# Two transformer blocks on one core: both tiles' x transposed unscaled, x^T of the first stage loaded as a second layout

## The chip, the cores and the metric

One core of one Trainium2 chip runs the whole program in one launch. The metric is the device time in microseconds, the median of three runs. The engines are named as in the profile: PE (TensorE) multiplies, PEld is its weight load, DVE (VectorE) and ACT (ScalarE) do elementwise work, POOL (GpSimd) a few small operations, and SP (SyncE) issues all DMAs, in order, on one queue.

## The reference

The input x has 256 tokens of width 1024, float32. It goes through two layers of a hybrid block and then two layers of a second block. Every sublayer has the same frame: a root mean square norm with a gain, one or more projections, some work of its own, an output projection, another norm with a gain, and the residual sum.

```python
def rms_norm(x, gain):
    xf = x.astype(jnp.float32)
    y = xf * lax.rsqrt(jnp.mean(xf * xf, axis=-1, keepdims=True) + EPS)
    return (y * gain.astype(jnp.float32)).astype(x.dtype)

def hybrid_layer(...):                      # two of these
    h = rms_norm(x, attn_pre_gain)
    u = h @ w_in                            # 4120 columns: q, k, v of two attentions, gates
    ...                                     # rope, sliding window attention with sinks, sparse attention
    mixed = sigmoid(g_a) * (o_a @ w_branch_a) + sigmoid(g_b) * (o_b @ w_branch_b)
    x = x + rms_norm(mixed @ w_out, attn_post_gain)
    h = rms_norm(x, ffn_pre_gain)
    x = x + rms_norm(conv_ffn(h, ...), ffn_post_gain)   # up 5632, causal conv of 3, gelu(a) * v, down
    return x

def second_block(...):                      # two layers of this
    f = _swiglu(_rmsnorm(x, g[0]), ...);  x = x + 0.5 * _rmsnorm(f, g[1])
    m = _mixer(_rmsnorm(x, g[2]), ...);   x = x + _rmsnorm(m, g[3])     # attention, short conv, pooling
    f = _swiglu(_rmsnorm(x, g[4]), ...);  x = x + 0.5 * _rmsnorm(f, g[5])
```

## The kernel before

The 256 tokens are two tiles of 128, called t = 0 and t = 1. There are ten stages: attention and FFN of layer 0 and 1, and then FFN, mixer, FFN of each layer of the second block. Both tiles go through all stages, the first a few weight units ahead of the second, so that the first tile's work of a stage fills PE while the second tile ends the stage before.

A product in float32 accuracy is made of three products of a fast format: each operand is split in a high part (a rounding copy on ACT) and a low part (the difference on DVE), and high x high, high x low and low x high are summed (`mm3`, lines 736 to 740). Weights come in units of 128 x 1024 float32 (512 KB): a DMA into one of three `raw` buffers, then `wh` on ACT and `wl` on DVE, into one of nine pairs (`loader`, `unit`).

A stage needs x^T, the model dimension on the partitions, as eight blocks `kt` of 128. `proj` uses x^T as the stationary operand and 512 weight columns as the moving one: eight blocks of three products for each tile. `proj_c` makes **joint products**: the weights stay, and both tiles' x^T, 256 columns, high and low side by side in the tile `xj`, move past them (lines 1508 and 1509). Since the norm's factor 1/rms belongs to a token, a product of `proj` can take it later, when its result leaves the accumulator (ACT's `scale`); a joint product has both tokens' tiles in its columns and needs x^T with 1/rms in it.

In the eight stages with joint products (`whole`: both FFNs and the mixer) the two tiles are made ready in two ways. Of the first tile x is transposed as it is as soon as it is written (`x_t`, line 787 does the transposing), goes into `xt[0]` as high and low, and feeds `proj`; beside that 1/rms is transposed to a row (line 857), and `times_row` makes x^T times 1/rms in `xj`. Of the second tile `x_normed` first makes 1/rms (two squares with sums on ACT, a power on POOL, line 776), multiplies x by it (line 513), and then transposes that straight into `xj`, from which both kinds of products read. In the attention stages both tiles are transposed as they are.

The program starts with loads of x in halves of 256 KB, of `first` (identity for the transposes, rope frequencies, gains) and of the first weights; PE begins with the sixteen transposes of x.

No engine's order is written out by hand. While the program is built, a planner (`_Order`) runs the stages as generators with a clock of its own: every instruction has an engine, a cost in a formula and a rank, and of those that are ready an engine takes the one of lowest rank. Ranks of this change: the transposes of x 1 to 1.3, 1/rms 1.5, `times_row` 3.2, a weight unit 4.5 or 7 by how soon it is needed, joint products 6. What comes out is fixed: on the chip each engine runs its list in order and waits for semaphores.

## Time and profile before

| | |
|---|---|
| median of 3 runs | 1708.73 us (1706.84 to 1711.24) |
| the profiled execution | 1708.78 us |
| its span, first to last instruction | 1706.8 us |
| instructions of PE, DVE, ACT, POOL | 8920, 2966, 2436, 56 |
| loaded | 302.26 MB, mean 177 GB/s |

A busy share is time in which an engine's rows cover the span. PE's rows overlap, since a product starts before the one in front has ended; the distance from start to start is what one more product costs. A wait is listed with what ended it. An instruction's idle time is what its engine stood still in front of it, so where PE waits the idle time and the distance of the two starts say nearly the same.

### The profile page before, as it was taken

How to read it: one execution, taken by the hardware profiler on the slowest of the kernel's cores; microseconds unless marked ns; L12 is line 12 of the kernel's file. 1: busy time of each engine (PE TensorE's matmuls, PEld its weight loads, DVE VectorE, ACT ScalarE, POOL GpSimd, SP SyncE). 2: the span in 40 equal slices, each digit the busy share in tenths (PEclk: the TensorE clock that was granted, in tenths of full speed). 3: DMA queues.
4: the chain of work that ended last, by engine and by line, in shares of the span. 5: the costliest groups of instructions: out<-in, count | busy, mean ns of one | idle time of the engine just before them, and what ended most of it. 6: DMA issues, size and time to landing. Idle time of an engine off the chain costs nothing.

```text
span 1706.8 us, 25832 instructions
## 1 busy us (share of the span) xinstructions
PE 1677.7 (98%) x8920; PEld 1391.8 (82%) x8920; DVE 1295.6 (76%) x2966; ACT 1078.6 (63%) x2436; POOL 40.5 (2%) x56
## 2 busy tenths in 40 slices
PE   8999999999999999999999999999999999999998
PEld 6778888888778888888888787888788887778887
DVE  7996898887977988896667878666776669776664
ACT  6665776677665866675556677555655556865553
POOL 0000000001000000000000000000000000000000
PEclk9999999999999999999999999999999999999999
DMA  7436555565246555556566545555665555446553
GB/s 242 156 103 219 177 182 184 187 202 180 94 147 192 173 185 189 191 180 203 165 195 198 173 148 174 176 183 191 201 186 163 192 189 178 154 160 193 178 185 111
DMA packets 85380, 302.26 MB, mean 177 GB/s; under 512 B 9984, under 2 KB 10240, under 8 KB 85248
## 3 DMA queue, kind: packets, MB, share of 16 engines
q1 hardware_dynamic: 85248, 300.60, 54.0%
q8 instruction: 70, 1.15, 0.3%
q14 instruction: 62, 0.51, 0.1%
HBM read 299.51 MB, written 1.05 MB: 176 GB/s over the span
## 4 chain that ended last, share of the span: by engine, by line
PE 77%; DVE 11%; DMA 5%; ACT 5%; issue 2%; POOL 0%; SPq 0%; DVEq 0%; POOLq 0%; ACTq 0%
PE bank L1508 24%; PE bank L1509 12%; PE bank L740 12%; PE bank L738 12%; PE bank L739 12%; DVE wl L502 4%; DMA raw<-in_w_dram 4%; DVE b L502 2%; PE bank L787 2%; ACT b L493 2%; ACT wh L493 2%; DVE x L506 1%; PE bank L1243 1%; ACT junk L493 1%; PE bank L1181 1%
## 5 line engine op out<-in xcount | busy, mean ns | idle before, releaser
L502 DVE TENSOR_TENSOR wl<-raw,wh 128x512 fp32r<-128x512 f32 x1096 | 721.6, 687 | 93.9 <-ACT wh L493 77.6
L493 ACT ACTIVATE wh<-raw 128x512 fp32r<-128x512 f32 x1096 | 641.9, 624 | 139.8 <-DMA raw<-in_w_dram 83.6
L1508 PE MATMUL bank<-xj,wh 128*128 128x512 f32 x1856 | 655.3, 397 | 2.1 <-ACT b L493 2.1
L1509 PE MATMUL bank<-xj,wl 128*128 128x256 f32 x1856 | 482.8, 281 | 0.0
L1508 PEld LDWEIGHTS bank<-xj,wh 128*128 128x128 f32 x1856 | 339.5, 188 | 69.3 <-ACT b L493 3.0
L1509 PEld LDWEIGHTS bank<-xj,wl 128*128 128x128 f32 x1856 | 350.1, 189 | 23.7
L493 ACT ACTIVATE b<-bank 128x256 f32<-128x256 f32 (+3 forms) x304 | 126.1, 418 | 302.6 <-PE bank L1508 278.7
L502 DVE TENSOR_TENSOR b<-b,bank 128x256 f32<-128x256 f32 x232 | 97.7, 421 | 207.5 <-ACT b L493 205.0
L738 PE MATMUL bank<-wh,r 128*128 128x512 f32 x528 | 208.7, 395 | 0.0
L740 PE MATMUL bank<-wh,r 128*128 128x512 f32 x528 | 206.3, 391 | 0.7 <-DVE r L502 0.6
L739 PE MATMUL bank<-wl,r 128*128 128x512 f32 x528 | 205.9, 390 | 0.0
L738 PE MATMUL bank<-wh,xj 128*128 128x512 f32 x400 | 165.9, 415 | 0.2
L740 PE MATMUL bank<-wh,xj 128*128 128x512 f32 x400 | 157.9, 395 | 1.8 <-DVE xj L506 1.8
L739 PE MATMUL bank<-wl,xj 128*128 128x512 f32 x400 | 156.8, 392 | 0.0
L738 PE MATMUL bank<-wh,xh 128*128 128x512 f32 x336 | 135.3, 403 | 0.0
L740 PE MATMUL bank<-wh,xl 128*128 128x512 f32 x336 | 131.8, 392 | 0.4 <-DVE xl L506 0.4
L739 PE MATMUL bank<-wl,xh 128*128 128x512 f32 x336 | 130.9, 390 | 0.0
L740 PEld LDWEIGHTS bank<-wh,r 128*128 128x128 f32 x528 | 99.1, 188 | 24.2 <-DVE r L502 2.7
L739 PEld LDWEIGHTS bank<-wl,r 128*128 128x128 f32 x528 | 99.3, 188 | 19.2
L738 PEld LDWEIGHTS bank<-wh,r 128*128 128x128 f32 x528 | 99.2, 188 | 18.3 <-ACT r L493 1.2
L740 PEld LDWEIGHTS bank<-wh,xj 128*128 128x128 f32 x400 | 75.4, 188 | 21.2 <-DVE xj L506 4.6
L493 ACT ACTIVATE r<-b 128x256 fp32r<-128x256 f32 (+1 forms) x128 | 55.6, 438 | 58.1 <-DVE b L502 40.5
(140 smaller groups left out, 1665.1 us busy)
## 6 DMA issues: line engine op xcount, KB each, us to landing
raw<-in_w_dram SPq DMA_DIRECT2D x547, 512.0 KB, 3.4
gp<-in_post_dram SPq DMA_DIRECT2D x10, 512.0 KB, 4.5
b<-in_w_dram SPq DMA_DIRECT2D x16, 256.0 KB, 5.5
x<-in_x_dram SPq DMA_DIRECT2D x4, 256.0 KB, 5.3
out_dram<-x SPq DMA_DIRECT2D x4, 256.0 KB, 2.0
small<-in_small_dram SPq DMA_DIRECT2D x1, 858.0 KB, 5.2
raw<-in_w_dram SPq DMA_DIRECT2D x2, 256.0 KB, 3.8
c<-in_const_dram SPq DMA_DIRECT2D x1, 292.0 KB, 4.2
```

Source lines behind the costliest of these rows:

```text
L493: return _Op("act", cost, lambda: self.nc.scalar.activation(out, in_, func, **kw), table or TABLE_OF.get(func))
L502: return _Op("dve", 0.069 + 0.00104 * _n(out), lambda: self.nc.vector.tensor_tensor(out, a, b, op=op))
L506: return _Op("dve", cost, lambda: self.nc.vector.scalar_tensor_tensor(out, in0=in0, scalar=scalar, in1=in1, op0=op0, op1=op1))
L738: mm(out, lhsT=ah, rhs=bh, start=start, stop=False)
L739: mm(out, lhsT=ah, rhs=bl, start=False, stop=False)
L740: mm(out, lhsT=al, rhs=bh, start=False, stop=stop)
L787: self.nc.tensor.transpose(ps[:, j * P:(j + 1) * P], s, self.ident)
L1181: nc.tensor.matmul(sb[i][:, 256 * k:256 * k + 256].rearrange("p (c k) -> p c k", c=2), lhsT=q[a][gs, j * P:(j + 1) * P], rhs=b[gs, br, slots],
L1243: nc.tensor.matmul(o[gs, oc:oc + 256], lhsT=vc, rhs=pT, start=n == 0 and c == 0, stop=br == 0 and n == chain[0] - 1 and c == 1)
L1508: both = lambda: nc.tensor.matmul(ps, lhsT=wh[:, c], rhs=self.xj2[:, kt], start=kt == 0, stop=kt == KT - 1)
L1509: low = lambda: nc.tensor.matmul(ps[:, 256:512], lhsT=wl[:, c], rhs=self.xj[0][:, kt], start=False, stop=False)
```

## The change

The second tile gets the first tile's way. `x_normed` and `scale` go; `x_t` transposes x as it is for both tiles into `xt[t]`; `proj` reads `xt[t]`; the evacuations of both tiles multiply by 1/rms and wait for it; the row of 1/rms and `times_row` are made for both tiles, of rank 2.8 now. The mixer's conv and pool parts, which write into `xt` later, wait for the input products of both tiles.

At the start x^T is a second input, laid out on the host as [128, 2048]. Four pieces of 256 KB are loaded and multiplied by the gain straight into `xj`, so that attention's first stage has no transposes of x; x itself is loaded behind them, for the norm and the residual. The gains come alone and first. PE gets eleven products on a zeroed tile, whose result nobody reads, in front of its first work. Three numbers of the planner are others: a DMA's landing 3.0 instead of 2.0, the power 0.95 instead of 0.6, and the loads of the post gains are put off by 40 or 20.

```diff
 def _layout(x):
+    a["xt"] = np.ascontiguousarray(a["x"].reshape(2, P, KT, P).transpose(3, 0, 2, 1).reshape(P, 2 * D))
...
-        self.row = self.sb([P, P], F32, "row")
+        self.row = self.sb([P, 2, P], F32, "row")
...
     def dma(self, out, in_, cost=0.1):
-        return _Op("dma", cost, lambda: self.nc.sync.dma_start(out=out, in_=in_), late=2.0)
+        return _Op("dma", cost, lambda: self.nc.sync.dma_start(out=out, in_=in_), late=3.0)
...
     def first_loads(self):
-        x(0, 0, 0)
-        order.go(load(self.first, self.d["first"], 0.45, "first"), 0.1)
-        x(0, 1, 0.3)
-        x(1, 0, 0.4)
-        x(1, 1, 0.6)
+        def x_t(t, h):
+            b = yield from self.one("b")
+            yield self.dma(b, self.d["xt"][:, D * t + 512 * h:D * t + 512 * h + 512], 0.73)
+            yield ("ev", "pre")
...
+                    yield self.cpa(self.xj[0][:, kt, s], src(kt), gain(kt))
...
+                    yield self.stt(self.xj[1][:, kt, s], src(kt), gain(kt), self.xj[0][:, kt, s].bitcast(F32),
+                                   ALU.mult, ALU.subtract)
...
+        def warm():
+            ps = yield from self.one("tr")
+            yield self.mset(self.junk, 0.0)
+            for _ in range(11):
+                yield self.pe(0.44, lambda: self.nc.tensor.matmul(ps, lhsT=self.junk[:, 0:P], rhs=self.junk,
+                                                                  start=True, stop=True))
+            self.free("tr", ps)
+        order.go(load(self.first[:, 0:10 * KT], self.d["first"][:, 0:10 * KT], 0.2, "pre"), 0)
+        order.go(x_t(0, 0), 0.2)
+        order.go(warm(), 0.1)
+        order.go(x_t(1, 0), 0.4)
+        order.go(x_t(0, 1), 0.55)
+        order.go(x_t(1, 1), 0.65)
+        order.go(load(self.first[:, 10 * KT:], self.d["first"][:, 10 * KT:], 0.3, "first"), 0.9)
+        x(0, 0.8)
+        x(1, 0.95)
...
     def norm_t(self, t, dst, gi, name, whole=False):
-        if whole and t:
-            self.order.go(self.x_normed(t, dst, gi, name), 1)
-            return
-        for q in range(4):
+        for q in range(4) if name != ("attn", 0) else ():
             self.order.go(self.x_t(t, q, dst, gi, name), 1 + 0.1 * q)
...
-                yield self.cp(self.row, ps[:, 0:P])
+                yield self.cp(self.row[:, t], ps[:, 0:P])
                 self.free("tr", ps)
                 for h in range(2):
-                    self.order.go(self.times_row(h, name), 3.2)
+                    self.order.go(self.times_row(t, h, name), 2.8)
...
-    def x_normed(self, t, dst, gi, name):
-        m = yield from self.one("m")
-        xn = yield self.get("b", 2)
...
-        yield from self.rstd(m)
-        for h in range(2):
-            yield self.ts(xn[h], half(h), m[:, 3:4])
-            self.order.set((name, "xn", t, h))
...
     def ffn_tile(self, l, i, t):
-        lhs = self.lhs_j(self.xj, t) if t else self.lhs_t(self.xt[0])
+        lhs = self.lhs_t(self.xt[t])
...
-            self.post_gain(n)
+            self.post_gain(n, 40.0)
...
     def glu_in(self, l, i, t, c, ps):
-        if t == 0:
-            yield ("ev", (name, "rs", t))
-        yield self.act(s[:, 0:256], ps[:, 0:256], AF.Silu, scale=self.scale(t))
-        yield self.stt(s[:, 256:512], ps[:, 256:512], self.scale(t), s[:, 0:256], ALU.mult, ALU.mult)
+        yield ("ev", (name, "rs", t))
+        yield self.act(s[:, 0:256], ps[:, 0:256], AF.Silu, scale=self.rs[t][:, 0:1])
+        yield self.stt(s[:, 256:512], ps[:, 256:512], self.rs[t][:, 0:1], s[:, 0:256], ALU.mult, ALU.mult)
...
     def mix_joint(self, l):
-            yield ("ev", (name, "in", 0, 2))
+            for t in range(2):
+                yield ("ev", (name, "in", t, 2))
...
-            self.order.go(self.loader(), lambda: (0.2, 0.5)[self.loaded] if self.loaded < 2 else 2)
+            self.order.go(self.loader(), lambda: (0.3, 0.5, 0.6, 0.7)[self.loaded] if self.loaded < 4 else 2)
```

What this does to the lists of the engines is shown at three places. The first is SP's list at the very start; x_122 and x_123 are the two tiles of x, raw_100 to raw_102 the weight buffers, and 128x512 of float32 are 256 KB. Before:

```order
1 L535 DMA x_122<-in_x_dram 128x512
2 L535 DMA first<-in_first_dram 128x272
3 L535 DMA raw_100<-in_w_dram 128x512 x2
4 L535 DMA x_122<-in_x_dram 128x512
5 L535 DMA x_123<-in_x_dram 128x512
6 L535 DMA raw_101<-in_w_dram 128x1024
7 L535 DMA x_123<-in_x_dram 128x512
8 L535 DMA pos<-in_positions_dram 128x1 x2
9 L535 DMA raw_102<-in_w_dram 128x1024
10 L535 DMA raw_100<-in_w_dram 128x1024
```

And now, with the pieces of x^T in the working buffers b_69 to b_72:

```order
1 L537 DMA first<-in_first_dram 128x80
2 L537 DMA b_69<-in_xt_dram 128x512
3 L537 DMA raw_100<-in_w_dram 128x512 x2
4 L537 DMA b_70<-in_xt_dram 128x512
5 L537 DMA raw_101<-in_w_dram 128x1024
6 L537 DMA b_71<-in_xt_dram 128x512
7 L537 DMA raw_102<-in_w_dram 128x1024
8 L537 DMA b_72<-in_xt_dram 128x512
9 L537 DMA x_122<-in_x_dram 128x1024
10 L537 DMA raw_100<-in_w_dram 128x1024
11 L537 DMA first<-in_first_dram 128x192
12 L537 DMA x_123<-in_x_dram 128x1024
```

The loads of x stand behind three weight units, and the fourth unit, the identity and the positions stand behind the first load of x.

The second place is PE's list where the second tile enters the mixer of the second block's first layer. r_88 feeds its last output product of the FFN in front, rs_129 and rs_130 are 1/rms of the two tiles, xh_125 and xl_126 the first tile's x^T, wh and wl weights, and b_79 and b_80 are the second tile's x times 1/rms. Before:

```order
4329 L740 MATMUL bank_62<-wh_119,r_88 128x512
4330 L857 MATMUL bank_66<-first,rs_129 128x128
...
4349 L787 MATMUL bank_65<-first,b_77 128x128 x4
...
4364 L740 MATMUL bank_63<-wh_109,xl_126 128x512
4365 L787 MATMUL bank_61<-first,b_79 128x128 x2
4366 L787 MATMUL bank_66<-first,b_79 128x128 x2
4367 L738 MATMUL bank_63<-wh_109,xh_125 128x512
...
4370 L787 MATMUL bank_67<-first,b_80 128x128 x2
4371 L738 MATMUL bank_64<-wh_111,xj 128x512
```

And now, where x_123 is the second tile's x, xh_127 its x^T, and line 1525 (1508 before) a joint product:

```order
4357 L785 MATMUL bank_64<-wh_103,r_88 128x512
...
4370 L832 MATMUL bank_63<-first,b_81 128x128 x4
...
4376 L785 MATMUL bank_66<-wh_117,xl_126 128x512
4377 L832 MATMUL bank_67<-first,x_123 128x128 x2
4378 L832 MATMUL bank_62<-first,x_123 128x128 x2
4379 L783 MATMUL bank_66<-wh_115,xh_125 128x512
...
4382 L832 MATMUL bank_61<-first,x_123 128x128 x2
...
4408 L832 MATMUL bank_63<-first,b_69 128x128 x4
4409 L890 MATMUL bank_67<-first,rs_130 128x128
...
4437 L785 MATMUL bank_62<-wh_117,xl_128 128x512
4438 L1525 MATMUL bank_66<-xj,wh_103 128x512
```

The second tile's transposes stand 18 products behind its last output product instead of 33; a second transpose of 1/rms is there, and 27 products later the first joint product.

The third place is DVE's list in the same stage change; m_98 and m_93 are the second tile's mean square before the power. Before:

```order
1722 L513 TENSOR_SCALAR m_98<-m_98 128x1
1723 L502 TENSOR_TENSOR xj<-b_76,xj 128x4x128
1724 L502 TENSOR_TENSOR b_75<-b_75,row 128x512
1725 L513 TENSOR_SCALAR b_79<-x_123,m_98 128x512
1726 L502 TENSOR_TENSOR wl_120<-raw_102,wh_119 128x512
1727 L513 TENSOR_SCALAR b_80<-x_123,m_98 128x512
1728 L502 TENSOR_TENSOR xj<-b_75,xj 128x4x128
1729 L502 TENSOR_TENSOR wl_120<-raw_102,wh_119 128x512
1730 L506 SCALAR_TENSOR_TENSOR xj<-bank_61,first,xj 128x128
```

And now, from the same point, with b_77 and b_80 the two halves of the second tile's x^T:

```order
1758 L515 TENSOR_SCALAR m_93<-m_93 128x1
...
1768 L519 COPY row<-bank_67 128x128
1769 L504 TENSOR_TENSOR wl_120<-raw_101,wh_119 128x512
1770 L504 TENSOR_TENSOR b_77<-xh_127,xl_128 128x512
1771 L504 TENSOR_TENSOR b_80<-xh_127,xl_128 128x512
1772 L504 TENSOR_TENSOR b_77<-b_77,row 128x512
1773 L504 TENSOR_TENSOR b_80<-b_80,row 128x512
1774 L504 TENSOR_TENSOR wl_120<-raw_101,wh_119 128x512
1775 L504 TENSOR_TENSOR wl_108<-raw_102,wh_107 128x512
1776 L519 COPY b_70<-bank_61 128x512
1777 L504 TENSOR_TENSOR xj<-b_77,xj 128x4x128
1778 L504 TENSOR_TENSOR xj<-b_80,xj 128x4x128
```

The two passes over x (b_79, b_80) are gone, and between the row and the second tile's xj stand two sums, two products and two differences, with weight passes among them.

## Rows read from the trace of the kernel before

**Rows 1.** The page, part 1: engine, busy us (share of the span), instructions
```profile
PE 1677.7 (98%) x8920; PEld 1391.8 (82%) x8920; DVE 1295.6 (76%) x2966; ACT 1078.6 (63%) x2436; POOL 40.5 (2%) x56
```

**Rows 2.** Waits of PE: engine, line, what ended them: us, times, longest
```profile
PE bank L787 <- DVE b L513: 5.6, 7, 1.4
PE bank L787 <- DMA first<-in_first_dram: 4.4, 1, 4.4
PE bank L787 <- DVE b L506: 4.0, 2, 2.2
PE bank L787 <- DMA x<-in_x_dram: 2.4, 1, 2.4
...
PE bank L740 <- DVE xj L506: 1.8, 5, 0.6
```

**Rows 3.** Timeline of the start: start, us, engine, line, tiles [idle before]
```profile
4.37 1.09 PE L787 MATMUL bank<-first,x 128*128 128x128 f32 x4 [4.37 <-DMA first<-in_first_dram]
...
5.07 1.31 ACT L493 ACTIVATE xj<-bank,first 128x128 fp32r<-128x128 f32 x4 [2.83 <-PE bank L787]
...
7.83 1.54 PE L787 MATMUL bank<-first,x 128*128 128x128 f32 x6 [2.38 <-DMA x<-in_x_dram]
...
9.03 0.78 PE L738 MATMUL bank<-wh,xj 128*128 128x512 f32 x1
...
9.60 0.63 PE L739 MATMUL bank<-wl,xj 128*128 128x512 f32 x1
...
12.87 0.74 PE L738 MATMUL bank<-wh,xj 128*128 128x512 f32 x1
...
13.44 0.40 PE L739 MATMUL bank<-wl,xj 128*128 128x512 f32 x1
```

**Rows 4.** Windows: length, PE, PEld, DVE, ACT, POOL busy, clock, DMA share
```profile
0.00:10.00 10.00, 3.26 (x12) 2.73 (x13) 2.31 (x7) 5.31 (x14) 0.20 (x4) 1.00 0.76 260
10.00:20.00 10.00, 10.00 (x41) 8.14 (x40) 9.71 (x35) 8.42 (x23) 1.10 (x2) 1.00 0.76 277
...
50.00:60.00 10.00, 9.09 (x71) 6.38 (x70) 8.49 (x31) 6.33 (x12) 0.00 (x0) 1.00 0.90 320
```

**Rows 5.** Chain of waits between 0 and 130 us: start us, us, what
```profile
44.68 5.42 DMA raw<-in_w_dram
...
53.84 5.49 DMA b<-in_w_dram
```

**Rows 6.** Timeline of a stage change of the second tile, 942 to 953 us
```profile
942.74 0.39 PE L740 MATMUL bank<-wh,r 128*128 128x512 f32 x1
...
946.88 0.75 DVE L506 SCALAR_TENSOR_TENSOR x<-b,m,x 128x512 f32<-128x512 f32 x1
...
948.14 0.74 DVE L506 SCALAR_TENSOR_TENSOR x<-b,m,x 128x512 f32<-128x512 f32 x1
...
950.36 1.46 POOL L776 TENSOR_TENSOR m<-m,half 128x1 f32<-128x1 f32 x1 [4.19 <-DVE m L513]
...
950.73 0.69 DVE L502 TENSOR_TENSOR b<-b,row 128x512 f32<-128x512 f32 x1
950.85 0.39 PE L740 MATMUL bank<-wh,xl 128*128 128x512 f32 x1
...
951.86 0.49 DVE L513 TENSOR_SCALAR b<-x,m 128x512 f32<-128x512 f32 x1 [0.44 <-POOL m L776]
...
952.40 0.66 PE L787 MATMUL bank<-first,b 128*128 128x128 f32 x4 [1.17 <-DVE b L513]
```

**Rows 7.** Instructions on the tile row: ns min/median/max, first and last start
```profile
L502 DVE TENSOR_TENSOR b<-b,row x16: 680/683/689, 198.5 to 1521.0; 128x512 f32<-128x512 f32 x16
L517 DVE COPY row<-bank x8: 279/282/286, 196.3 to 1516.4; 128x128 f32<-128x128 f32 x8
```

**Rows 8.** Line 857: the same columns
```profile
L857 PE MATMUL bank<-first,rs x8: 271/271/272, 195.6 to 1515.5; 128*128 128x128 f32 x8
```

**Rows 9.** Instructions on the tile x: the same columns
```profile
L513 DVE TENSOR_SCALAR b<-x,m x16: 473/481/488, 203.6 to 1525.8; 128x512 f32<-128x512 f32 x16
```

More of the change, by code (lines that the diff above doesn't have):

```diff
@@ L630, in load, with x, whole @@
             order.set(name)
-        def x(t, h, rank):
-            c = slice(512 * h, 512 * h + 512)
-            order.go(load(self.x[t][:, c], self.d["x"][t * P:(t + 1) * P, c], 0.73, ("x", -1, t, h)), rank)
-        x(0, 0, 0)
-        order.go(load(self.first, self.d["first"], 0.45, "first"), 0.1)
-        x(0, 1, 0.3)
-        x(1, 0, 0.4)
-        x(1, 1, 0.6)
+        def x(t, rank):
+            def whole():
+                yield self.dma(self.x[t], self.d["x"][t * P:(t + 1) * P, :], 1.45)
+                for h in range(2):
+                    order.set(("x", -1, t, h))
+            order.go(whole(), rank)
@@ new lines, in x_t, with highs, lows @@
+        def x_t(t, h):
+            b = yield from self.one("b")
+            yield self.dma(b, self.d["xt"][:, D * t + 512 * h:D * t + 512 * h + 512], 0.73)
+            yield ("ev", "pre")
+            s = slice(t * P, t * P + P)
+            kts = range(4 * h, 4 * h + 4)
+            src, gain = (lambda kt: b[:, (kt % 4) * P:(kt % 4) * P + P]), (lambda kt: self.p["pre"][:, kt:kt + 1])
+            def highs():
+                for kt in kts:
+                    if (t, kt) == (0, 2):
+                        yield ("ev", (("in", 0, "kA", 0), 512))
+                    yield self.cpa(self.xj[0][:, kt, s], src(kt), gain(kt))
+                    order.set(("xh", t, kt))
+            def lows():
+                for kt in kts:
+                    yield ("ev", ("xh", t, kt))
+                    yield self.stt(self.xj[1][:, kt, s], src(kt), gain(kt), self.xj[0][:, kt, s].bitcast(F32),
+                                   ALU.mult, ALU.subtract)
+                    order.set((("attn", 0), "kt", t, kt))
+            yield ("par", [highs(), lows()])
+            self.free("b", b)
@@ L641, in first_loads @@
+        order.go(warm(), 0.1)
[5 more added lines that the diff above has]
+        x(1, 0.95)
         yield self.mset(self.half, -0.5)
-        yield self.act(self.junk[:, 0:1], self.half, AF.Sin)
+        yield self.act(self.small_out, self.half, AF.Sin)
         for t in range(2):
-            order.go(load(self.pos[:, t:t + 1], self.d["positions"][t * P:(t + 1) * P, :], 0.45, ("pos", t)), 0.7)
+            order.go(load(self.pos[:, t:t + 1], self.d["positions"][t * P:(t + 1) * P, :], 0.45, ("pos", t)), 0.97)
@@ L703, in loader @@
             self.loaded = n + 1
-            self.order.go(self.unit(key, raw, late), lambda n=n: 4.5 if n - self.unit_now < SOON else 7)
+            self.order.go(self.unit(key, raw, late), lambda n=n: 0.15 if n == 0 else 4.5 if n - self.unit_now < SOON else 7)
     def unit(self, key, raw, late):
@@ L813, in x_t @@
             self.order.set((name, "kt", t, kt))
-            if src is not None:
-                self.order.set((name, "jt", t, kt))
         self.free("tr", ps)
@@ L877, in times_row, with post_gain @@
         yield self.tt(b3, hi, lo, ALU.add)
-        yield self.tt(b3, b3, self.row[:, None, :].to_broadcast([P, 4, P]), ALU.mult)
-        yield from self.split(self.xj[0][:, k, 0:P], self.xj[1][:, k, 0:P], b3)
+        yield self.tt(b3, b3, self.row[:, t, None].to_broadcast([P, 4, P]), ALU.mult)
+        s = slice(t * P, t * P + P)
+        yield from self.split(self.xj[0][:, k, s], self.xj[1][:, k, s], b3)
         self.free("b", b)
         for kt in kts:
-            self.order.set((name, "jt", 0, kt))
-    def scale(self, t, n=1.0):
-        return n if t else self.rs[t][:, 0:1] if n == 1.0 else self.rs[t][:, 2:3]
-    def x_normed(self, t, dst, gi, name):
-        m = yield from self.one("m")
-        xn = yield self.get("b", 2)
-        for q in range(4):
-            self.order.go(self.x_t(t, q, dst, gi, name, xn[q // 2]), 1 + 0.1 * q)
-        half = lambda h: self.x[t][:, 512 * h:512 * h + 512]
-        for h in range(2):
-            yield ("ev", ("x", self.prev(name), t, h))
-            yield self.square(half(h), m[:, h:h + 1])
-        yield from self.rstd(m)
-        for h in range(2):
-            yield self.ts(xn[h], half(h), m[:, 3:4])
-            self.order.set((name, "xn", t, h))
-        self.free("m", m)
-    def post_gain(self, n):
+            self.order.set((name, "jt", t, kt))
+    def post_gain(self, n, after=0.0):
         def load():
+            yield ("sleep", after)
             gp = yield from self.one("gp")
@@ L1829, in mix_pool @@
         self.free("b", p0, s0, s1)
-        yield ("ev", (name, "in", 0, 2))
+        for t in range(2):
+            yield ("ev", (name, "in", t, 2))
         yield ("par", [self.split(ct[t][0][:, 6 + a], ct[t][1][:, 6 + a], po[:, t * P:t * P + P],
@@ L1836, in phases @@
     def phases(self, t, n):
-        yield ("ev", "first")
         todo = []
```

46 lines of the change are left out of this document (19 added, 27 removed).

## The prediction

> **What bounds the kernel now.** Read the busy shares first, then what TensorE (PE) waits for, then the two places where those waits lie. PE is busy for 1677.7 of 1706.8 us, DVE for 1295.6 [rows 1]. A change that leaves PE's products alone can therefore take back only PE's waits and its slow start. The profile's list of PE's waits has ten lines; those that this change can touch are the start (4.4 for `first` and 2.4 for x), 5.6 us in seven waits of line 787 for line 513, 4.0 in two waits of line 787 for a scalar_tensor_tensor on tile b, and 1.8 in five waits of line 740 for xj [rows 2].
>
> Line 787 is the transposing helper, line 513 on b is the second tile's x times 1/rms. The timeline of one stage change shows how they hang together [rows 6]: x of the second tile is complete at 948.88 (948.14 + 0.74), but its transposes start at 952.40, behind the squares, the power on POOL (1.46) and the scaling (0.49). PE's last product before them began at 950.85. Line 513's rows on x are 16: eight stages, two halves each [rows 9]. No line of the list has PE waiting for x as DVE writes it, although the first tile is transposed straight from x in all eight stages, and both tiles in the attention stage.
>
> At the start, products last 0.63 up to 12.87 and 0.40 from 13.44 [rows 3]: the two clock levels of PE, 1.2 and 2.4 GHz, with sparse work from 4.37 and close work from 7.83 in front of the rise. Seven of the 512-column products are done before 13.44 (the first at 9.03, the last at 12.87).
>
> **The change part by part.** The profiled execution took 1708.78 us, beside its span of 1706.8; the median of the three runs is 1708.73, so the sum stands against 1708.8.
>
> (a) Start. Sixteen transposes vanish and x^T arrives ready, so that a product needs a transfer, one ACT pass and one DVE pass. At full rate products follow each other by 0.23 (950.62 to 950.85 in the stage shown). The old start is thus worth a gapless row of products from 13.44 - 7 x 0.23 = 11.8. In the new order the second tile's first piece closes a queue of 40 + 256 + 512 + 256 = 1064 KB; the old one had 256 + 136 + 512 + 256 = 1160 KB when the wait for x ended at 7.83 [rows 3]. At the same rate that is 7.2 to 7.8; with a gain pass (1.31 for four, so 0.33, [rows 3]) and its rest on DVE, 8.3 to 8.5. One triple of the first tile (0.7) is done by then: a gapless row from about 7.6, 4.2 us sooner. That is PE's bound. DVE's is other: it is busy 9.71 of the second ten us and 8.49 of the sixth [rows 4], and the chain passes through weight loads of 5.42 and 5.49 there [rows 5]. DVE works only 2.31 of the first ten; the new start fills some of that, but x comes twice (1 MB more, about 3.3 us at the 0.3 MB per us of those windows), and weights wait for that. Ends: 0 and -4.2; a slow clock would add: if eleven idle products don't raise it, some ten products at 0.43 instead of 0.23 cost 2. I take -2.0, nearer to DVE's bound because DVE is the full engine there.
>
> (b) The waits for the scaled x vanish. 5.6 for line 513 and 1.8 for xj behind it, in twelve waits [rows 2]. The list counts idle time after the modelled end: in the stage shown it says 1.17, where the distance of the starts is 1.55, less 0.23 = 1.32 [rows 6]. So 0.15 more for each: 7.4 + 12 x 0.15 = -9.2.
>
> What is late next: x itself. In the mixer the new order puts the second tile's transposes 18 products and 4 transposes behind its last output product, 18 x 0.23 + 4 x 0.11 = 4.6 us. The trace has that product at 942.74 and the first half of x at 946.88 + 0.75 = 947.63, 4.9 later [rows 6]. That is a wait of about 0.3, and as much can come in each of the eight: +2.4. Ends: 0, since the first tile shows none, and 8 x 1.2, the wait that is there now.
>
> (c) The two waits of 2.0 each for a scalar_tensor_tensor [rows 2] are in the gated FFN, where DVE had other work of the stage change in front. The change reorders just this, but adds work for DVE too. Ends: -4.0 and +2 (half as much again); I take -2.0.
>
> (d) Eight transposes of 1/rms more. One such takes 0.27 [rows 8] and 0.11 of PE's row; between the two, 8 x 0.12 = +1.0.
>
> (e) x times 1/rms for the second tile. Each stage gains six DVE passes of 0.68 and a copy of 0.28, and loses two of 0.48 [rows 7, 9]: 3.4, so 27 us over the kernel. DVE has 411 free; this lies beside PE as long as xj is ready when the joint products begin. In the mixer's new order 27 products and four transposes stand between the row's transpose and the first joint product: 6.7 us. On DVE the row's copy and nine passes stand up to xj's first half: 0.28 + 9 x 0.69 = 6.5, and the copy starts 0.3 after the transpose. So about 0.2 short in each: +1.6. Ends: 0 and 8 x 1.4, two weight passes that slip in front. ACT gains one pass of 512 columns for each half; it is 63% busy [rows 1].
>
> (f) The second tile's evacuations now wait for its 1/rms. Queued behind them on ACT are weight conversions; eleven us of the tile's own products run meanwhile (16 triples of 0.69), and 1/rms needs about 4 us from x (948.88 to 951.82, the power's end, and three small passes) [rows 6]. Cost 0; without that cover it would be the wait for the power. The mixer's conv and pool parts wait for the second tile's input products as well, work of rank below the attention: 0. The post gain loads come 20 or 40 us later, over 50 us before they are used, and no line of PE's waits names a weight load in these stages: 0. The planner's new costs (a transfer's landing, the power) issue nothing.
>
> One rule speaks against (e). The power that took 1.46 ran while DVE had a pass with two SBUF inputs, 950.73 to 951.42 [rows 6]. The Trainium skill, "SBUF — State Buffer", section "SBUF: two separate sides", says that such a pass and a GpSimd op that reads SBUF take one port pair in turn, each for its whole length. By the rule alone each stage has its power later by a pass of DVE, since (e) adds six such passes; this row agrees. Whether it costs anything is (f)'s question, and a rival below.
>
> The sum: -2.0 - 9.2 + 2.4 - 2.0 + 1.0 + 1.6 = -8.2, so 1700.5.
>
> **The rivals.** All of it: the start is PE's (-4.2), x is never late, both waits of (c) go, (e) fits. -4.2 - 9.2 - 4.0 + 1.0 = -16.4: 1692.4. For it speaks that the first tile never waits for x; against it the full DVE of the start.
>
> The wait only moves: x is late by 0.8 in each stage as DVE is busier there (6.4 instead of 2.4), the start gives nothing, and (c) stays. -9.2 + 6.4 + 1.0 + 1.6 = -0.2: 1708.6; half of it, 1704.6. For it speaks that DVE in the stage change already holds x back to 4.9 us behind the last product.
>
> 1/rms late: the power is held up by one more pass of 0.69 in each of eight stages, the evacuations are late by that, no bank is free, and PE stands. 1700.5 + 8 x 0.69 = 1706.0. Against it speak the eleven us of (f).
>
> Slower: DVE becomes the bound of each stage change. Its place is the first joint product, which now needs the second tile's xj. If DVE takes two more weight passes and a power first (2 x 0.69 + 1.46 = 2.8) and the reserve is the 0.2 above, 8 x 2.8 = 22 on top: 1722. It eats the gain from 1.0 in each stage on and decides from 1.7. Against it: the rank of these passes is raised above the weights' (2.8 against 4.5 or 7).
>
> **How the numbers follow.** The forecast 1700.5, with 1696 to 1703.5 as its own range: 0.58. All of it: 0.16. The wait only moves: 0.16; 1/rms late: 0.05; slower: 0.05. A measurement of this kernel tells 0.3%, 5.1 us, from no change: below 1703.6 is faster. The first two are (0.74), with a little of the third at its half-way point (0.02): 0.76 faster. The rest of the third and 1/rms late, 0.19, are within; 0.05 slower. The range 1692.5 to 1707 leaves out about 0.08 below and 0.12 above.
>
> **What would show it.** (a) right: products at 0.40 from about 8, no transposes of x at the start, and the attention of layer 0 some 2 us sooner; wrong: products of 0.63 after 9, or waits of PE for wl or raw before 60. (b) right: line 513 gone from PE's list, and waits for x of at most 0.5; wrong: a line of PE's transposes waiting for x of 5 us or more. (e) wrong: the joint line waiting for xj in most stages. (c): the line on b by scalar_tensor_tensor below 3. The forecast is wrong as a whole if the start's gain, read at the end of the first layer, is 0 and the x waits sum to 6.

## The result, and the profile after

The changed kernel takes 1689.79 us (median of 4 runs, 1689.16 to 1690.41) beside 1707.78 for the kernel before on the same chip (1706.59 to 1711.24): ratio 0.9891, interval 0.9874 to 0.9908. That is 18.0 us faster, where the forecast was 8.2, and below its range, which began at 1692.5. The profiled execution took 1689.79 us with a span of 1688.0.

The page, part 1 and the heads of its part 4 (the chain that ended last), which answers to [rows 1]:

```profile
PE 1674.6 (99%) x8923; PEld 1390.9 (82%) x8923; DVE 1318.0 (78%) x3031; ACT 1085.7 (64%) x2452; POOL 41.4 (2%) x56
...
PE 85%; DVE 11%; ACT 3%; issue 1%; DMA 0%; SPq 0%; DVEq 0%; POOLq 0%; ACTq 0%
```

The same head of the chain before:

```profile
PE 77%; DVE 11%; DMA 5%; ACT 5%; issue 2%; POOL 0%; SPq 0%; DVEq 0%; POOLq 0%; ACTq 0%
```

PE is busy for 3 us less and DVE for 22 more, so most of what went is idle time of PE: span less busy time was 29.1 us and is 13.4. The chain hints at where it had come from: before it ran 77% over PE and 5% over DMAs, now 85% and nothing. The waits of PE, which answer to [rows 2] (the transposing helper is line 832 now, the products are 783 to 785, the joint products 1525 and 1526):

```profile
PE bank L783 <- ACT wh L495: 1.5, 1, 1.5
PE bank L832 <- DVE b L504: 1.3, 4, 0.5
PE bank L785 <- DVE xl L508: 1.2, 3, 0.6
PE bank L673 <- DVE half L534: 1.2, 1, 1.2
PE bank L785 <- DVE r L504: 0.5, 2, 0.3
PE bank L832 <- DVE b L508: 0.3, 1, 0.3
```

The line for x times 1/rms is gone, the 4.0 for a scalar_tensor_tensor on b is 0.3, and no line has PE waiting for x; xl, the low part of x^T, costs 1.2 (0.4 before). A line of the list before is gone too, which the forecast had left out as out of reach:

```profile
PE bank L1508 <- ACT b L493: 2.1, 2, 1.1
```

The start, PE's timeline, and the same stretch by windows (length, PE, PEld, DVE, ACT, POOL busy, granted clock, DMA share, GB/s), beside [rows 3, 4]:

```profile
1.19 3.98 PE L673 MATMUL bank<-junk 128*128 128x512 bf16 x11 [1.19 <-DVE half L534]
6.65 0.50 PE L783 MATMUL bank<-wh,xj 128*128 128x512 f32 x1 [1.49 <-ACT wh L495]
...
8.28 0.63 PE L783 MATMUL bank<-wh,xj 128*128 128x512 f32 x1
...
10.46 0.62 PE L785 MATMUL bank<-wh,xj 128*128 128x512 f32 x1
10.89 0.43 PE L783 MATMUL bank<-wh,xj 128*128 128x512 f32 x1
11.16 0.39 PE L784 MATMUL bank<-wl,xj 128*128 128x512 f32 x1
```

```profile
6.00:8.00 2.00, 1.12 (x3) 0.58 (x3) 1.75 (x4) 1.61 (x5) 0.00 (x0) 0.88 0.95 378
8.00:10.00 2.00, 2.00 (x6) 1.36 (x5) 1.45 (x5) 2.00 (x8) 0.00 (x0) 0.50 0.98 386
10.00:12.00 2.00, 2.00 (x8) 1.59 (x7) 2.00 (x6) 2.00 (x7) 0.00 (x0) 0.76 1.03 417
```

Real products begin at 6.65, the first still at the high level (0.50 long). Then the granted clock falls to 0.50, the level of 1.2 GHz, and products last 0.63 until 10.89: PE had been idle for 1.49 behind the eleven idle products. Before 13.46 twenty products have begun, where the old start had seven.

The second tile's stage change, the same as [rows 6] 5.3 us earlier:

```profile
941.56 0.74 DVE L508 SCALAR_TENSOR_TENSOR x<-b,m,x 128x512 f32<-128x512 f32 x1
...
942.70 0.60 PE L832 MATMUL bank<-first,x 128*128 128x128 f32 x4
942.83 0.74 DVE L508 SCALAR_TENSOR_TENSOR x<-b,m,x 128x512 f32<-128x512 f32 x1
...
943.49 1.28 DVE L504 TENSOR_TENSOR xj<-b,xj 128x512 fp32r<-128x512 f32 x2
...
944.69 0.68 DVE L504 TENSOR_TENSOR wl<-raw,wh 128x512 fp32r<-128x512 f32 x1
...
945.29 0.34 DVE L508 SCALAR_TENSOR_TENSOR xl<-bank,first,xh 128x128 fp32r<-128x128 f32 x1
...
945.69 0.50 PE L785 MATMUL bank<-wh,xl 128*128 128x512 f32 x1 [0.33 <-DVE xl L508]
...
947.79 1.46 POOL L821 TENSOR_TENSOR m<-m,half 128x1 f32<-128x1 f32 x1 [6.94 <-DVE m L515]
```

The transposes begin 0.40 behind x (942.30 to 942.70), in front of the power instead of behind it, and PE waits 0.33 in all. That wait isn't for x: between x and the first xl DVE has the first tile's two xj passes and a weight pass. The added DVE passes stand in tile row's two lines, twice as many as in [rows 7] at the same length:

```profile
L504 DVE TENSOR_TENSOR b<-b,row x32: 676/681/686, 194.9 to 1515.5; 128x512 f32<-128x512 f32 x32
L519 DVE COPY row<-bank x16: 274/280/286, 192.8 to 1512.8; 128x128 f32<-128x128 f32 x16
```

To see where the time went, read one instruction that both traces have in each stage: the first tile's first sum into x. Its start in us, and how far four other kernels (below) stand from the kernel before there:

| end of stage | before | after | after − before | e10 | e5 | e3 | e2 |
|---|---|---|---|---|---|---|---|
| attention 0 | 186.81 | 183.46 | −3.4 | −1.7 | +1.3 | +2.6 | −0.4 |
| attention 1 | 555.53 | 552.19 | −3.3 | −1.6 | +3.3 | +3.3 | +0.4 |
| FFN 1 | 746.47 | 742.25 | −4.2 | −2.3 | +4.3 | +3.0 | +0.7 |
| swiglu | 933.47 | 927.11 | −6.4 | −4.4 | +3.5 | +3.3 | −0.2 |
| mixer | 1031.02 | 1021.92 | −9.1 | −7.1 | +0.2 | +2.2 | −1.3 |
| swiglu | 1409.03 | 1395.12 | −13.9 | −11.9 | −2.0 | +1.4 | −3.3 |
| last | 1694.27 | 1675.23 | −19.0 | −16.9 | −6.7 | +0.5 | −4.0 |

The gain comes in two pieces: 3.4 before the first stage's end, and 14.8 in the six stages of the second block, 2.5 in each. The rest of layers 0 and 1 gives 0.9. Column e5, the changed kernel with one planner's number put back, is 4.3 behind the kernel before at FFN 1 and then gains 11.0 in the second block. (These are single executions, on several chips, and by the last row some 3 us off what the ratios say (e3: +0.5, and 2.6 faster by its ratio); the ratios below, each a run's time over that of the kernel before on the same chip, with a 95% interval, come from runs side by side.)

### The profile page after: what moved, and what is told of

It reads as the page before. It is cut to its first block, busy times and chain, and to the rows that moved or that the text cites. A ratio compares the mean times of both kernels' runs of the same rounds, so it can differ in the third digit from the quotient of the medians.

```text
span 1688.0 us, 25864 instructions
## 1 busy us (share of the span) xinstructions
PE 1674.6 (99%) x8923; PEld 1390.9 (82%) x8923; DVE 1318.0 (78%) x3031; ACT 1085.7 (64%) x2452; POOL 41.4 (2%) x56
## 4 chain that ended last, share of the span: by engine, by line
PE 85%; DVE 11%; ACT 3%; issue 1%; DMA 0%; SPq 0%; DVEq 0%; POOLq 0%; ACTq 0%
PE bank L1525 25%; PE bank L783 14%; PE bank L785 14%; PE bank L784 14%; PE bank L1526 13%; DVE b L504 3%; DVE wl L504 3%; PE bank L832 2%; DVE b L508 1%; ACT b L495 1%; PE bank L1260 1%; ACT wh L495 1%; DVE b L519 1%; DVE x L508 1%; PE bank L1198 1%
## 5 line engine op out<-in xcount | busy, mean ns | idle before, releaser
L504 DVE TENSOR_TENSOR wl<-raw,wh 128x512 fp32r<-128x512 f32 x1096 | 720.5, 685 | 71.0 <-ACT wh L495 55.3
L495 ACT ACTIVATE b<-bank 128x256 f32<-128x256 f32 (+3 forms) x286 | 116.3, 417 | 280.4 <-PE bank L1525 267.0
L783 PE MATMUL bank<-wh,xh 128*128 128x512 f32 x480 | 194.8, 406 | 0.0
L785 PE MATMUL bank<-wh,xl 128*128 128x512 f32 x480 | 188.1, 392 | 1.2 <-DVE xl L508 1.2
L784 PE MATMUL bank<-wl,xh 128*128 128x512 f32 x480 | 187.5, 391 | 0.0
L783 PE MATMUL bank<-wh,xj 128*128 128x512 f32 x256 | 106.9, 418 | 1.5 <-ACT wh L495 1.5
L785 PEld LDWEIGHTS bank<-wh,xl 128*128 128x128 f32 x480 | 90.1, 188 | 22.1 <-DVE xl L508 2.5
L783 PEld LDWEIGHTS bank<-wh,xh 128*128 128x128 f32 x480 | 90.3, 188 | 17.1
L784 PEld LDWEIGHTS bank<-wl,xh 128*128 128x128 f32 x480 | 90.5, 188 | 15.7
L784 PE MATMUL bank<-wl,xj 128*128 128x512 f32 x256 | 101.0, 394 | 0.2 <-DVE wl L504 0.2
```

The costliest lines, as they stand in the source:

```text
L495: return _Op("act", cost, lambda: self.nc.scalar.activation(out, in_, func, **kw), table or TABLE_OF.get(func))
L504: return _Op("dve", 0.069 + 0.00104 * _n(out), lambda: self.nc.vector.tensor_tensor(out, a, b, op=op))
L783: mm(out, lhsT=ah, rhs=bh, start=start, stop=False)
L784: mm(out, lhsT=ah, rhs=bl, start=False, stop=False)
L785: mm(out, lhsT=al, rhs=bh, start=False, stop=stop)
```

## Experiments: the parts one by one

The change has three parts: the start, the second tile's way, and the planner's numbers. Each is put in or left out alone. The edits are abridged to what tells a run from its neighbours.

**e1, the start alone.** On the kernel before:

```diff
-        x(0, 0, 0)
...
+        order.go(x_t(0, 0), 0.2)
+        order.go(warm(), 0.1)
...
```

> The kernel before with the new start alone (x^T as a second layout, gains first, eleven idle products, x behind them); the second tile keeps x times 1/rms before its transposes, and the planner's numbers are the old ones. Theory, the start is worth what the two traces show at the first sum into x (183.46 against 186.81): 3.4 us sooner at that place and 3.4 at the end, about 1704.5. Rival (the forecast's term, DVE and the weights behind it bound the start): 2.0 or less, 1705.8 to 1708. Second rival: the place is reached 3.4 sooner but the order of later stages comes out otherwise, so that the end moves by another number, 0 to 6.

Measured: 1.0028 (1.0018 to 1.0038), slower. Neither the theory nor its rivals: by its trace it is 1.6 behind at the end of attention 0, and 9.0 at the end. Its list of PE's waits has 3.8 in four for ACT on r, which the kernel before doesn't have; that these are the whole loss isn't shown.

**e2, the second tile's way alone.**

```diff
-            self.order.go(self.x_normed(t, dst, gi, name), 1)
...
+        for q in range(4):
+            self.order.go(self.x_t(t, q, dst, gi, name), 1 + 0.1 * q)
```

> The kernel before with the second tile's new way alone (transposed as it is, 1/rms at the evacuation, times_row for both tiles at the old rank 3.2); the old start and the old planner's numbers. Theory: the stage changes give what the waits of PE in the trace before name (5.6 + 1.8 and 0.15 for each of 12: 9.2) less the 2.0 by which x itself is late after: 7.2, and the two waits for a scalar_tensor_tensor on b (4.0) and the two for a bank (2.1 at the joint products, line 1508) go only with the planner's numbers: 1700.5. Rival: those waits go with the new way itself: another 6, 1694.5.

Measured: 0.9971 (0.9958 to 0.9983), 5.0 us, and 4.0 by the trace. The theory's 7 was a little high. The two waits on b go with the new way itself (1.2 in four is left), but 3.2 in six waits for ACT on r, 2.6 in four for x and 2.0 in two for xj at the joint line come in their place.

**e3, both without the numbers.**

```diff
-late=3.0
+late=2.0
-_Op("pool", 0.95,
+_Op("pool", 0.6,
-self.post_gain(n, 40.0)
+self.post_gain(n)
-self.times_row(t, h, name), 2.8
+self.times_row(t, h, name), 3.2
```

> The changed kernel with the planner's numbers put back (a DMA's landing 2.0, the power 0.6, post gains not put off, times_row at 3.2). Theory: the waits of 4.0 for a scalar_tensor_tensor on b and of 2.1 for a bank come back, about 1695.5. Rival: the numbers issue nothing and cost nothing, as the forecast has it: 1689.8.

Measured: 0.9985 (0.9975 to 0.9994). The whole change without its four numbers is worth 2.6 us instead of 18. Far worse than the theory, and far from the rival, which was the forecast's own step.

**e4, the numbers alone**, on the kernel before. The rank 2.8 is in it too, for the first tile's times_row, which the expectation doesn't name:

```diff
-late=2.0
+late=3.0
-_Op("pool", 0.6,
+_Op("pool", 0.95,
-self.post_gain(n)
+self.post_gain(n, 40.0)
-self.times_row(h, name), 3.2
+self.times_row(h, name), 2.8
```

> The kernel before with the planner's new numbers alone (landing 3.0, power 0.95, post gains put off by 40 and 20, nothing else). Theory: 4.0 and 2.1 of PE's waits go, the waits for x times 1/rms stay: about 1702. Rival: no difference, 1707.8.

Measured: 0.9959 (0.9944 to 0.9973), 7.0 us. The waits for x times 1/rms stay (6.7 in six), as expected; those on b shrink to 0.9, but those for a bank (2.1) stay.

**e9 and e10, the numbers with the start, and with the second tile's way**, each on the changed kernel:

```diff
+        if whole and t:                       # e9
+            self.order.go(self.x_normed(t, dst, gi, name), 1)
+            return
...
-        order.go(x_t(0, 0), 0.2)              # e10
+        x(0, 0, 0)
...
```

> The new start with the planner's new numbers, the second tile in its old way. Theory: with a landing of 3.0 the start keeps the 3.4 us that the trace of the changed kernel shows at the first sum into x; on top of the numbers alone (0.9959) that is 0.994. Rival: the start costs time with this landing too, as it did with 2.0 (1.0028): 0.997 or more.

> The second tile's new way with the planner's new numbers, the old start. Theory: the rest of the gain is here, 9 us on top of the numbers alone: 0.9905. Rival: the new way is worth what it was with the old numbers (5 us, 0.9971), 0.993, and only the three together reach 0.989.

Measured: e9 0.9955 (0.9943 to 0.9968), e10 0.9891 (0.9878 to 0.9905). The second tile's way with the numbers has the whole gain; the start adds nothing that the timing tells. By the single traces it keeps 1.7 us to 2.1 from the first stage to the last (1677.33 in e10 against 1675.23).

## Experiments: which number, and why

**e5 to e8, e11 to e14, one number each in the changed kernel.** `late` is what the planner adds to a transfer's own 1.45 until it has landed.

```diff
-late=3.0                    # e5: 2.0   e12: 2.5   e11: 3.4   e8: 4.0
+late=2.0
-self.post_gain(n, 40.0)     # e6
+self.post_gain(n)
-0.95 and rank 2.8           # e7
+0.6 and rank 3.2
```

> The changed kernel with one number put back: the planner lets a DMA land 2.0 after its issue instead of 3.0. Theory: this number carries most of what the numbers are worth together (0.9891 with them, 0.9985 without), because with it ACT stands in front of a weight transfer that has not landed, with the stage change's work queued behind: ACT's waits for raw rise from 54 us towards the 103 of the kernel without the numbers, and the ratio to the kernel before is 0.996 or more (1701 beside 1708). Rival: another number carries it, and the ratio stays at 0.989 to 0.991.

> The changed kernel with the post gains loaded at once, not 40 or 20 us later. Theory (landing number): within 2 us of the changed kernel, ratio 0.988 to 0.991. Rival: the gains' 512 KB in the stage change hold the weights up by the 4.7 us that such a load takes in the trace, in eight stages, some of it in front of PE: ratio 0.993 or more.

> The changed kernel with the power's cost back at 0.6 and times_row back at rank 3.2. Theory (landing number): within 2 us of the changed kernel, 0.988 to 0.991. Rival: the waits for xj at the joint products (2.0 in two waits where the new way ran with the old numbers) come back through the rank: 2 to 4 us, 0.9905 to 0.992.

> The changed kernel with a landing of 4.0. The trace has 3.4 us as the median from a weight unit's issue to its landing, so 3.0 is still short for most of them. Theory: ACT's waits for raw fall from 54 us to under 40, and the end comes 0 to 5 us sooner than with 3.0 (ratio 0.986 to 0.989). Rival: the order that came out at 3.0 was a lucky one, and any other number gives one to five us back, 0.990 to 0.992.

> The changed kernel with a landing of 3.4, the median that the trace has for a weight unit. Theory (the number should be the true one): as good as 3.0 or better, 0.986 to 0.989. Rival (each number gives another order, and that of 3.0 is lucky): anywhere between 0.991 and 1.002, the two ends seen at 2.0 and 4.0.

> The changed kernel with a landing of 2.5. Theory (the number should be the true one): between 2.0 and 3.0 in ACT's waits for raw (93 and 54 us) and in time (0.9958 and 0.9888): about 0.992. Rival (lucky order): not in order with its neighbours, 0.996 or more.

e13 and e14 split the landing between the weight units and all other transfers:

```diff
-                late, op.late = op.late, 0.0
+                late, op.late = 3.0, 0.0      # e13, all others 2.0
+                late, op.late = 2.0, 0.0      # e14, all others 3.0
```

> The changed kernel; the planner lets weight units land 3.0 after their transfer's own 1.45, all other DMAs 2.0. In the trace half of the weight units take more than 3.45 us from issue to landing and one in seven more than 4.45. Theory: it is the weights that matter, ACT stands before a unit that is late; ratio as with 3.0 for all, 0.988 to 0.990. Rival: the other transfers (x^T, constants, the small tables of the first 80 us) matter, 0.994 or more.

> The other half: weights land at 2.0, all other DMAs at 3.0. Theory: as with 2.0 for all, ACT waits over 85 us for raw, ratio 0.994 to 0.997. Rival: 0.988 to 0.990.

| landing | 2.0 (e5) | 2.5 (e12) | 3.0 (after) | 3.4 (e11) | 4.0 (e8) | weights 3.0 (e13) | others 3.0 (e14) |
|---|---|---|---|---|---|---|---|
| ratio | 0.9958 | 0.9918 | 0.9891 | 0.9897 | 1.0017 | 0.9901 | 0.9944 |
| ACT waits for raw, us | 93.1 | 81.9 | 54.0 | 42.9 | 60.6 | 56.5 | 93.4 |

The half width of each ratio is 0.001 to 0.002. e6 gave 0.9888 and e7 0.9892: beside a landing of 3.0 the post gains, the power and the rank do nothing that the timing tells. Beside 2.0 the three together do: e3 and e5 differ in these three alone, 0.9985 and 0.9958. The landing of the weights carries most of the number's worth (e13 against e14). Two of the expectations speak of 3.4 us as the true landing and of 3.0 as short; that was a misreading, since the planner adds the transfer's own 1.45: 2.0 stands for 3.45 us from issue to landing, 3.0 for 4.45. The trace of before has a median of 3.5 for raw, between 3.0 and 6.2; of its 549 loads 50% take over 3.45, and 13% over 4.45. So with 2.0 every second weight load takes longer than the list of ACT was made for. What that does, in e5, ACT and PE in one place:

```profile
247.24 0.63 ACT L503 ACTIVATE wh<-raw 128x512 fp32r<-128x512 f32 x1 [1.00 <-DMA raw<-in_w_dram]
...
247.78 0.58 ACT L503 ACTIVATE b<-b,small 128x256 f32<-128x256 f32 x1
...
248.27 0.40 ACT L503 ACTIVATE r<-b 128x256 fp32r<-128x256 f32 x1
...
248.72 0.50 PE L802 MATMUL bank<-wh,r 128*128 128x512 f32 x1 [1.07 <-ACT r L503]
```

ACT stands 1.00 in front of a weight load. Behind it in ACT's list is the r that PE needs next, and PE stands 1.07. The list names ACT on r as the releaser; the cause is the load two instructions ahead. In e3, where all four numbers are back, it takes one step more, over ACT, DVE and PE:

```profile
1229.70 0.63 ACT L503 ACTIVATE wh<-raw 128x512 fp32r<-128x512 f32 x1 [0.81 <-DMA raw<-in_w_dram]
1230.24 0.58 ACT L503 ACTIVATE junk<-bank 128x512 bf16<-128x512 f32 x1
...
1230.94 0.69 DVE L512 TENSOR_TENSOR b<-bank,gp 128x512 f32<-128x512 f32 x1 [1.38 <-ACT junk L503]
...
1234.93 0.75 DVE L516 SCALAR_TENSOR_TENSOR x<-b,m,x 128x512 f32<-128x512 f32 x1
...
1235.73 0.66 PE L851 MATMUL bank<-first,x 128*128 128x128 f32 x4 [1.58 <-DVE x L516]
```

The late load is in front of a square (junk) that DVE waits 1.38 for; DVE doesn't stand again until x, and PE stands 1.58 for x. The waits of ACT for raw, in the kernel before, after, and in e5:

```profile
ACT wh L493 <- DMA raw<-in_w_dram: 83.6, 80, 4.0
```

```profile
ACT wh L495 <- DMA raw<-in_w_dram: 54.0, 57, 2.8
```

```profile
ACT wh L503 <- DMA raw<-in_w_dram: 93.1, 82, 3.1
```

Time follows them from 2.0 to 3.0 (e12 met its forecast of 0.992), is flat to 3.4, and at 4.0 it doesn't: ACT's waits are 60.6 there, and PE waits 1.9 in seven for wl and 3.7 in six for r in the mixer's attention (line 1796). The theory that a larger number is only safer fell with e8; what it changes in the order, and why that costs over 20 us, stays open. ACT's waits also order only kernels that are otherwise alike: e4 and e9, with the second tile's old way, have 31.3 and 28.6 and are slower than the changed kernel.

Where the number's worth lies can be read from column e5 of the table beside that of the changed kernel: of the 12.3 us between the two traces 4.6 are there at the end of attention 0, 3.9 come in the rest of layers 0 and 1, and 3.9 in the second block.

**e16, a try for a better version:** landing 3.4, and x taken as ready later.

```diff
-XWAIT = 0.3
+XWAIT = 0.9
```

> The changed kernel with a landing of 3.4 and x held ready 0.9 instead of 0.3 after its sum is issued, as the planner sees it. With 3.4 alone the kernel led by 2.5 us up to the first swiglu stage and then lost 7 where PE waited four times for x (0.6 each, and the granted clock fell to half for 3.4 us behind two of them). Theory: with x later in the plan PE has other products there, and the lead stays: ratio 0.987 to 0.9885, better than any so far. Rival: the transposes move behind products that the second tile needs sooner, xl comes late instead, and nothing is won: 0.989 to 0.991.

Measured: 0.9902 (0.9888 to 0.9915), the rival: the waits for x are gone, and 2.6 for xl and 1.4 for xj stand in their place. No version beat the changed kernel by more than the noise; e6 equals it.

## Experiments: what bounds the stage change

**e15, one DVE pass twice**, each engine's order else unchanged:

```diff
         yield self.tt(b3, hi, lo, ALU.add)
+        # second tile only: issued twice, the planner counts it once
```

> The changed kernel with the sum of high and low in times_row issued twice for the second tile (16 more DVE passes of 0.6, each result the same; every engine's order is otherwise that of the changed kernel). In its trace the first joint product of the eight stages starts 1.66, 1.66, 5.45, 0.24, 0.5, 0.06, 0.24 and 0.5 us after the second tile's first half of xj is ready. Two passes more in front of it are 1.2. Theory (the reserve is what the trace shows): 0 in the three first stages and 0.96, 0.7, 1.14, 0.96, 0.7 in the others, 4.5 in all, ratio 0.9915, with PE's waits for xj at the joint line. Rival: DVE has room and makes the passes good before they are needed, 0.989. Second rival: DVE bounds each stage change, all 16 passes show, 9.6 us: 0.9945.

Measured: 0.9950 (0.9937 to 0.9964), 10 us more than the changed kernel, as the second rival has it. The theory's own part is exact and not the whole:

```profile
PE bank L1590 <- DVE xj L513: 3.8, 5, 1.4
PE bank L805 <- DVE r L513: 1.7, 3, 1.2
PE bank L852 <- ACT b L504: 1.5, 4, 0.5
PE bank L804 <- DVE wl L513: 1.5, 4, 0.5
PE bank L852 <- DVE b L513: 1.4, 4, 0.5
```

Five waits at the joint line: by the distance of the same rows in both traces 0.53, 1.07, 1.44, 0.53 and 1.00, 4.6 where 4.5 was worked out. The rest comes as waits for r, for wl and in front of transposes, in the other three stages as well. Read at the table's row, each of the eight stages with the doubled pass is 1.1 to 1.5 us longer than in the changed kernel, where its two passes are 1.2; the two attention stages, which have none, are −0.5 and 0.0. So in the stage change DVE has no room, though it is 78% busy over the span and PE waits little for it. The windows say it too, one stage change before and the same after (columns as above):

```profile
1216.00:1256.00 40.00, 37.36 (x176) 30.00 (x175) 33.26 (x72) 26.27 (x64) 3.49 (x4) 1.00 0.59 185
```

```profile
1205.00:1245.00 40.00, 39.41 (x187) 31.72 (x187) 36.55 (x82) 27.81 (x67) 4.03 (x4) 1.00 0.51 172
```

The change took 2 us of PE's idle time there and filled DVE from 83 to 91%.

**e17 and e18, passes taken off DVE:** the sum goes to POOL, for both tiles and for the first alone.

```diff
-        yield self.tt(b3, hi, lo, ALU.add)
+        yield self.tt(b3, hi, lo, ALU.add, "pool")                     # e17
+        yield self.tt(b3, hi, lo, ALU.add, "dve" if t else "pool")     # e18
```

> The changed kernel with the sum of high and low in times_row on POOL for both tiles, 32 passes of 0.6 less on DVE (19 us, all in stage changes). POOL's products of 256 columns take 0.90 in the trace and those of 192 0.75, so a sum of 512 should take about 1.7 (0.29 and 0.0024 for each column). Theory (DVE at its limit there, PE not far from its own): PE gets back what it still waits for in the stage changes, 1.2 for xl, 1.3 and 0.3 for b, about 3 us, ratio 0.987. Rival: the second tile's sum is 1.1 longer on its way and its reserve at the joint products is 0.06 to 0.5, so that PE waits there, 5 stages by 0.6 to 1.0: 0.991. Second rival: while POOL sums, DVE's passes with two inputs stand, 32 by 1.7: DVE loses more than it gains, 0.995 or more.

> The same for the first tile alone: 16 passes of 0.6 less on DVE (9.6 us), and the second tile's way to xj as it is. Theory: if taking off were the mirror of adding (16 passes cost 10.4 us) this would give 10; but PE's waits in the stage changes are only about 3, so 1 to 3 us, ratio 0.987 to 0.9885. Rival (the DVE passes stand while POOL sums, 16 by 1.7): 0.993 or more. Second rival: nothing, 0.989 to 0.990, since PE was the bound in the changed kernel.

Measured: e17 0.9948 (0.9936 to 0.9961), e18 0.9895 (0.9880 to 0.9910). The second rival of e17, and nothing gained in e18. POOL and DVE in e17:

```profile
1222.46 1.57 POOL L512 TENSOR_TENSOR b<-xh,xl 128x512 f32<-128x512 f32 x1
...
1228.52 1.75 POOL L512 TENSOR_TENSOR b<-xh,xl 128x512 f32<-128x512 f32 x1
```

```profile
1223.10 1.47 DVE L513 TENSOR_TENSOR wl<-raw,wh 128x512 fp32r<-128x512 f32 x1
...
1224.81 0.68 DVE L513 TENSOR_TENSOR wl<-raw,wh 128x512 fp32r<-128x512 f32 x1
...
1229.03 1.79 DVE L513 TENSOR_TENSOR b<-b,row 128x512 f32<-128x512 f32 x1
```

A pass of 0.68 takes 1.47 and 1.79 while POOL sums. Over the span the wl passes are 738.4 busy instead of 720.5, and those with row 30.2 instead of 21.8: 26 us lost where 19 were taken off. In e18 the passes with row and some wl passes are held up in the same way (wl 730.6), and the time still doesn't change; so neither run tells what DVE's passes would be worth without POOL in their way.

## Why the prediction missed

**The step that failed is "The planner's new costs (a transfer's landing, the power) issue nothing."** They issue nothing and order everything. With the landing put back to 2.0 the change gives 0.9958, 7 us (e5); the other 11 hang on that one number, and with all four back 2.6 are left (e3). That e5's 7 is about what the forecast gave to the whole is luck: by the table e5 is 4.3 behind the kernel before at the end of layer 1, where the forecast had −2.0 for the start, and it gains 11.0 in the second block, where the terms (b) to (e) sum to −6.2.

The forecast read the new order, which the numbers had already made, in one place, and was right about it; then it took the middle of its bounds for most terms, since something would be late next. With the old numbers something is: in e3 PE waits 3.9 for ACT on r, 3.0 for x and 2.0 for xj, and the second block gains 2.5. With the new ones little is, it gains 14.8, and the terms come out near their far ends. The trace of before had the clue: ACT waited 83.6 us for raw, and DMAs held 5% of the chain.

**(a), the start, −2.0.** Its size fits the single traces (e10 against after: 1.7 to 2.1); the ratios of the two, both 0.9891, don't tell it from 0. That PE doesn't bound the start holds, as the forecast had it: with the clock low until 10.89 or at its high level from 6.7 on (e7, where PE waited for wl instead), attention 0 ends at 183.46 and 183.43. What the term was to show, products of 0.40 from about 8, came at 10.9, and its sign of being wrong, products of 0.63 after 9, is there. Without the landing number the start costs time (e1).

**(b), −9.2 and +2.4.** The waits went. With the old numbers x itself is late as forecast, by 2.6 and 3.0 (e2, e3); in the changed kernel PE never waits for it. What is there is 0.8 more for xl, in three stages, where DVE is full.

**(c), −2.0,** was mis-sized: 4.0 became 0.3. The same holds for a wait that had no term at all, 2.1 for a bank at the joint products; e2, e5 and e10 have none of it, e1, e4 and e9 have it, so it goes with the second tile's way.

**(d)** is there: sixteen transposes of 1/rms where there were eight, none waited for.

**(e), +1.6,** cost nothing, though its place was right: the forecast had xj 0.2 short in each stage (its own numbers, 0.3 + 6.5 − 6.7, make it 0.1); the trace after has it 0.06 to 0.5 early in five stages and 1.7, 1.7 and 5.5 in three. e15 shows that DVE has nothing to spare beyond that. The slower rival, DVE as the bound of each stage change, named the right place; its price begins with the next pass.

**(f)** cost nothing in its waits for 1/rms: no line of PE's list names them. What was said against (e) is seen in e17, where a DVE pass of 0.68 with two inputs in SBUF took 1.79 beside a sum on POOL. The Trainium skill, "SBUF — State Buffer", section "Who interferes with whom", says that a DVE instruction with two SBUF inputs and a GpSimd instruction that reads SBUF contend, and that the port pair is locked for one of them. e17 agrees, 0.68 became 1.79. In the changed kernel it decides little, since POOL is busy there for 41.4 us in all.

By the terms, with the waits as measured and the forecast's own price for (a) and (d): −2.0 − 9.2 + 0.8 − 3.7 − 2.1 + 1.0 + 0 = −15.2, of the 19.0 between the two traces. The remaining 3.8 are in no term. Of them 1.4 come before the end of attention 0, where e10, with the old start, leads by 1.7 as well; what they are stays open. How much of each term belongs to the numbers and how much to the second tile's way can't be told apart by sums: alone the two give 7.0 and 5.0 us (e4, e2), together 18.6 (e10).

## What to carry to other kernels

Where a planner fixes the order, its cost for a transfer is part of the kernel: don't set it to the median load, and time a few larger values. Here 4.45 us, in which 87% of the loads have landed by the trace of before, was among the best, and 5.45, in which 98% have, lost over 20 us. Don't price a change of such a number at nothing; look at the waits of the engine that stands in front of loads. An engine that waits little and is waited for little can still have no room in one stage; double a pass there, with the order held, before counting on its idle share. Before moving a pass from DVE to POOL, see whether DVE has passes with two inputs in SBUF at the times when POOL would run it.

## What the runs showed of the hardware

The granted clock fell behind short waits of PE. In e8 PE waited 0.78 and 1.77 between 216 and 219.4, and the windows of the next 7 us are at 0.51:

```profile
213.00:219.00 6.00, 3.88 (x19) 2.74 (x17) 6.00 (x15) 5.28 (x11) 0.00 (x0) 1.00 0.25 87
219.00:222.00 3.00, 2.57 (x5) 1.66 (x6) 3.00 (x8) 3.00 (x7) 0.00 (x0) 0.51 0.19 41
222.00:226.00 4.00, 4.00 (x11) 3.10 (x10) 4.00 (x11) 2.47 (x6) 0.00 (x0) 0.51 0.97 351
226.00:230.00 4.00, 4.00 (x22) 3.33 (x21) 2.98 (x6) 1.46 (x3) 0.00 (x0) 1.00 0.48 152
```

From 222 to 226 PE's products stand 0.43 apart, from 226 on 0.23. At the start the eleven idle products last 3.90 to 4.66 us together where the clock rose among them, and 4.87 or 4.88 where it had not risen by their end. Where it was up and PE then stood for 1.49 (the changed kernel), 1.54 (e6), 1.42 (e9) or 1.19 (e14) behind them, it fell; where PE stood for 1.10 (e3) or 1.04 (e16), it stayed up. In e1 and e7 it rose only about the end of a wait of 0.51 and 0.49. In e5 it had not yet risen, and products ran 0.43 apart until 10.55, though PE was idle for only 0.61. None of it shows at the end of attention 0, where the changed kernel and e7 differ by 0.03.
